# Small loads issued from GpSimd's queue, and the read-out of the memory's keys spread behind the first query unit in other PSUM banks: a one-core decoder trunk

## The chip, the core and the metric

The kernel runs on one NeuronCore of a Trainium2 chip. The metric is the device time of one execution in microseconds (us); the time of a kernel is the median of its runs. Engines are named as in the profile: PE (TensorE), DVE (VectorE), ACT (ScalarE), POOL (GpSimd) and SP (SyncE, which here only issues loads). Each engine, and each engine's queue of DMA issues, works through its own instructions in a fixed order.

## What is computed

One sandwich-normalised layer on 256 tokens of width 2048 in float32: the input is normalised and projected, four branches (causal pooling, dilated window attention, chunked gated linear attention, attention into 256 memory tokens) work on parts of the projection, sigmoid gates mix their outputs, and one output projection is normalised and added to the input.

```python
h = rms_norm(x, g_pre[l])
proj = h @ w_in[l]
(a_val, a_gate, sq, sk, sv, s_gate, cq, ck, cv, c_gate, c_lr,
 mq, m_gate, g_logits) = jnp.split(proj, split_at, axis=-1)
y_a = pool_mixer(a_val, a_gate, w_pool[l], pool_scale[l])
...
y_m = mem_attn(mq, m_gate, mem, g_mem[l], w_mem_kv[l])   # keys km, values vm = rms_norm(mem, g_mem) @ w_mem_kv
gates = jax.nn.sigmoid(g_logits.reshape(B, S, N_BRANCH, D_MODEL) + b_merge[l])
merged = (gates[:, :, 0] * (y_a @ w_br_pool[l]) + ... + gates[:, :, 3] * (y_m @ w_br_mem[l]))
x = x + rms_norm(merged @ w_out[l], g_post[l])
```

## The kernel before

Every float32 matmul operand is split in two: a high part (ACT copies the tile to the narrower matmul type) and a low part (DVE subtracts the high part from the tile). `split_w` (L134) does this for half a weight tile of 128x2048, which `load_raw` (L129) has fetched by SP's queue into one of 13 buffers (`raw`). Names end in `h` and `l` for the two parts: `cq10h` and `cq10l` are the first half of the unit `cq1`. High and low parts have five buffers each. PE then multiplies high by high, high by low and low by high.

A `b_unit` (L174) loads one weight tile, splits each half, and issues 16 matmuls a half, pairs of one with 512 and one with 256 columns; its result is read from PSUM by `two_sums` (L193): one copy on ACT (`cq1s`), one addition on DVE (`gq` for queries).

The head of the program, where most of the change lies:

- `mem_chunk(0)` to `mem_chunk(3)` (L305): the memory tokens (`mr`, with parts `mhl`) times the weights of the values (`vma`, two PSUM banks) and of the keys (`kma`, four banks). The sums of squares of the memory go to `msq`.
- `x_prep` (L286), woven in between by a list of generators (`queue`, of which `pull` runs one step): loads x in four tiles `xn`, adds up squares in `xsq`, works out the inverse norms (`inv_rms`, L244: matmuls `xpc`, a power on POOL, matmul `xpr`, a copy), scales x by 16 instructions of L297, and splits it into `xhl`.
- After chunk 3, L353 to L356 read out the four key banks (`km0s` to `km3s` with an addition each) and the two value banks.
- Then the query units `cq0` to `cq3` and the key units `ck0` to `ck3` (L640 on) of the linear attention, with three generators pulled in between: `bias_prep` (L384: POOL clears `braw`, SP loads the merge biases into it, `brow` and `sel` are made), `quarter_prep` (L362: eight differences `qs` of quarters of x, each split into a `quarter` tile, for the gate matmuls), and `m_norm` (L269: the memory's inverse norms `mcol` and `mrow`; `vm` and `km` are scaled by them). `drain("quarters")` before `ck0` runs what is left of the biases and quarters.
- From `ck0` on, the gate matmuls (`gu`, `gt`, `gv`, L409) fill PE between all other units.

SP also fetches `walpha` and `big_cst` (L480, L482; constants first used far later) and, near the end, the four pooling weights `wpr` (L805). The branch matmuls of the tail (`bmem`, `bswa`, ...) come from L902 on.

PSUM has the tags `sm` (2 banks), `acc` (2) and `seven` (4). Before, values lie in `seven`, keys in two `seven` and two `acc` banks; `b_unit` takes its bank from `acc`.

Of the kernel before, what the change touches and what calls it, by code (L numbers as in the profile page):

```python
# [8 lines left out]
F32 = mybir.dt.float32  # L9
R = mybir.dt.float32r  # L10
AF = mybir.ActivationFunctionType
ALU = mybir.AluOpType
# [25 lines left out]
def kernel(ctx, tc, ins, out):  # L38
# [83 lines left out]

    raw_count = [0]

    def new_raw():
        raw_count[0] += 1
        return e8(f"raw{raw_count[0]}", [P, 2048])

    def load_raw(src, n):  # L129
        raw = new_raw()  # L130
        sync.dma_start(raw[:, :n], src[:, :n])
        return raw

    def split_w(raw_ap, n, name):  # L134
        hi = wp.tile([P, 1024], R, tag="hi", bufs=NB_HILO, name=name + "h")
        lo = wp.tile([P, 1024], R, tag="lo", bufs=NB_HILO, name=name + "l")
        act.activation(hi[:, :n], raw_ap, AF.Copy)  # L137
        vec.tensor_tensor(lo[:, :n], raw_ap, hi[:, :n].bitcast(F32), op=ALU.subtract)
        return hi, lo

    def mm3(o, sh, sl, wh, wl, start=False, stop=False, again=False):
# [29 lines left out]

        return finish

    def b_unit(name, src, mov, evac):  # L174

        a = acc(f"{name}a", [P, 512])
        raw = load_raw(src, 2048)
        for hf in range(2):
            hi, lo = split_w(raw[:, hf * 1024 : (hf + 1) * 1024], 1024, f"{name}{hf}")
            for kk in range(8):  # L180
                k = 8 * hf + kk
                ws = slice(kk * P, (kk + 1) * P)
                mh, _ = mov(k)
                ten.matmul(a[:], lhsT=hi[:, ws], rhs=mov.both(k), start=(k == 0), stop=False)  # L184
                ten.matmul(a[:, :T], lhsT=lo[:, ws], rhs=mh, start=False, stop=(k == KT - 1))
            if hf == 0:
                pull(1)
                gates(2.8)
        evac(name, a)
        pull(1)  # L190
        gates(2.8)
# [48 lines left out]
    def fold(sq):  # L240
        vec.tensor_tensor(sq[:, 0, 0:2], sq[:, 0, 0:2], sq[:, 0, 2:4], op=ALU.add)
        vec.tensor_tensor(sq[:, 0, 0], sq[:, 0, 0], sq[:, 0, 1], op=ALU.add)

    def inv_rms(name, sq, col, row):  # L244

        fold(sq)
        yield
        pc = sm(f"{name}pc", [P, 2, 2])
        for t in range(2):
            ten.matmul(pc[:, t, :], lhsT=sq[:, 0, 0, t * P : (t + 1) * P], rhs=ones[:, 0:2], start=True, stop=True)  # L250
        vec.tensor_scalar(col, pc[:, :, 0], 1.0 / D, EPS, op0=ALU.mult, op1=ALU.add)
        pool.tensor_tensor(col, col, half[:], op=ALU.pow)
        dg = c2(f"{name}dg", [P, T])
        for t in range(2):
            vec.tensor_scalar(dg[:, t * P : (t + 1) * P], ident[:], col[:, t : t + 1], None, op0=ALU.mult)
        yield
        pr = sm(f"{name}pr", [P, T])
        ten.matmul(pr[:], lhsT=ones[:], rhs=dg[:], start=True, stop=True)
        vec.tensor_copy(row, pr[:])
# [7 lines left out]
    vm = c4("vm", [P, 2, 512])  # L267

    def m_norm():  # L269
        yield from inv_rms("m", msq, mcol[:], mrow)  # L270
        yield
        for t in range(2):
            act.activation(vm[:, t, :], vm[:, t, :], AF.Copy, scale=mcol[:, t : t + 1])
        yield
        for h in range(4):
            vec.tensor_tensor(km[:, h, :], km[:, h, :], mrow, op=ALU.mult)
        yield
# [8 lines left out]
    def x_prep():  # L286
        for c in range(4):
            xn.append(c4(f"xn{c}", [P, 4, T]))
            sync.dma_start(xn[c][:], ins["xT"][:, 4 * c : 4 * c + 4, :])
            squares(xsq, xn[c], c)  # L290
            yield
        yield from inv_rms("x", xsq, xcol[:], xrow)
        yield
        for c in range(4):
            for i in range(4):
                k = 4 * c + i
                vec.scalar_tensor_tensor(xn[c][:, i, :], xn[c][:, i, :], g_pre[:, k : k + 1], xrow,  # L297
                                         op0=ALU.mult, op1=ALU.mult)
            put_hilo(h_at.four(c, 0), h_at.four(c, 1), xn[c][:])
            yield  # L300

    vm_acc = [seven(f"vma{t}") for t in range(2)]
    km_acc = [seven(f"kma{h}") if h < 2 else acc(f"kma{h}", [P, 512]) for h in range(4)]

    def mem_chunk(c):  # L305

# [21 lines left out]
        for j in range(2048 // n):  # L328
            hi, lo = split_w(rv[:, j * n : (j + 1) * n], n, f"vm{c}{j}")
            for i in range(n // 512):  # L330
                k, ws = (n // 512) * j + i, slice(i * 512, (i + 1) * 512)
                for t in range(2):
                    ts = slice(t * P, (t + 1) * P)
                    mm3(vm_acc[t][:], hl[:, k, 0, ts], hl[:, k, 1, ts], hi[:, ws], lo[:, ws],
                        c == 0 and k == 0, c == 3 and k == 3)
            if n * (j + 1) % 1024 == 0:
                pull(1)
        squares(msq, rawx, c)
        for j in range(2):
            hi, lo = split_w(rk[:, 1024 * j : 1024 * j + 1024], 1024, f"km{c}{j}")  # L340
# [9 lines left out]
    queue.append(("xprep", x_prep()))  # L350
    for c in range(1, 4):
        mem_chunk(c)
    for h in range(4):  # L353
        two_sums(f"km{h}", km_acc[h], km[:, h, :])
    for t in range(2):
        act.activation(vm[:, t, :], vm_acc[t][:], AF.Copy)  # L356
    drain("xprep")


    quarter = [e8(f"quarter{i}", [P, 2, 8, P], R) for i in range(4)]  # L360
# [23 lines left out]
    def bias_prep():  # L384
        raw = c2("braw", [48, 512])
        pool.memset(raw[:], 0.0)
        rows = ins["b_merge"].rearrange("b (j c) -> (b j) c", c=512)
        sync.dma_start(raw[0:16, :], rows)
        sync.dma_start(raw[32:48, :], rows)
        act.activation(brow[:], raw[:], AF.Copy)  # L390
        vec.tensor_tensor(brow[32:48, :], raw[32:48, :], brow[32:48, :].bitcast(F32), op=ALU.subtract)
        one = c2("bsel", [48, 24])
        vec.tensor_tensor(one[:, 0:16], ident[0:48, 0:16], ident[0:48, 32:48], op=ALU.add)
        two = one[:, 0:16].rearrange("p (r i) -> p r i", i=2)
        vec.tensor_tensor(one[:, 16:24], two[:, :, 0], two[:, :, 1], op=ALU.add)
        vec.tensor_copy(sel[:], one[:])
        yield
# [70 lines left out]
    def all_gates():  # L468
        for jj in range(2):
            for b in range(4):  # L470
                yield from gate_pair(b, jj)

    queue.append(("quarters", bias_prep()))
    queue.append(("quarters", quarter_prep()))
    queue.append(("mnorm", m_norm()))
# [1 line left out]
    vec.tensor_scalar(g_gla, g_gla, 0.5, None, op0=ALU.mult)  # L477
    vec.tensor_scalar(p_scale, p_scale, 0.5, None, op0=ALU.mult)
    walpha = cst.tile([16, 512], F32, name="walpha")
    sync.dma_start(walpha[:], ins["w_alpha"])  # L480
    big_cst = cst.tile([P, 1344], F32, name="big_cst")
    sync.dma_start(big_cst[:], ins["consts"])  # L482
    dist0 = big_cst[:, 0:384].rearrange("p (g j) -> p g j", g=3)
    dist1 = big_cst[:, 384:1152].rearrange("p (g j) -> p g j", g=3)
    amask = big_cst[:, 1152:1280]
# [152 lines left out]
    vec.tensor_copy(ones_r[:], ones[:])  # L638

    for h in range(4):  # L640
        b_unit(f"cq{h}", ins["w_cqk"][h], h_at, plain_evac(gq[:, h, :], SCALE))
    drain("quarters")
    gate_stream[0] = all_gates()
    for h in range(4):
# [157 lines left out]

    def mix(g):
        wr = c2(f"wpr{g}", [P, 512])
        sync.dma_start(wr[:], ins["w_pool"][g])  # L805
        yield from pool_group(g)
        hi, lo = split_w(wr[:], 512, f"wpl{g}")
        yield
# [244 lines left out]
```

## Time and profile before

| | |
|---|---|
| median of 3 runs | 1206.92 us (1206.21 to 1209.74) |
| the profiled execution's own time | 1205.37 us |
| its span | 1203.5 us, so 1.9 us lie around it |
| instructions | 15395 |
| PE busy | 1161.6 us (97%), 5846 matmuls |
| DVE / ACT / POOL busy | 962.8 (80%) / 648.4 (54%) / 51.2 us (4%) |
| TensorE's granted clock over the span | 0.987 of full speed |
| DMA | 301.84 MB, 251 GB/s on average; SP's queue 62.3% of the 16 engines' time |
| chain that ended last | PE 69%, DVE 7%, DMA 5%, issue 2%, ACT 2% |

PE is busy for all but 42 us of the span. A gap is read in the view of waits and in the timeline: a number in brackets is how long the engine was idle before the row's instruction, and behind the arrow stands what ended that idle time. The clock is read in the windows (column PEclk) and in the distance between the starts of equal matmuls.

### The profile page before, as it was taken

What the parts mean: (1) busy time and instruction counts of PE and PEld (TensorE: products, weight loads), DVE (VectorE), ACT (ScalarE), POOL (GpSimd) and SP (SyncE); (2) the same over time, 40 slices, a digit from 0 to 9 for tenths busy, and PEclk for the clock granted to TensorE, in tenths of its full rate; (3) what the DMA queues carried; (4) which work ended last, traced back from release to release, by engine and by line L of the source; (5) the groups of instructions that cost most, each with busy time, mean ns of one, the idle gap of its engine ahead of it and who ended that gap; (6) DMA issues with size and microseconds to landing.
All of it is one profiled execution on the core that took longest, in us unless ns stands there. A gap on an engine that the chain in (4) does not pass through costs nothing.

```text
span 1203.5 us, 15395 instructions
## 1 busy us (share of the span) xinstructions
PE 1161.6 (97%) x5846; PEld 975.2 (81%) x5846; DVE 962.8 (80%) x1197; ACT 648.4 (54%) x823; POOL 51.2 (4%) x96
## 2 busy tenths in 40 slices
PE   9779999999999999999999999999999989999997
PEld 7558888878888878888888888888887868888787
DVE  6857978899799799789789968988987677776454
ACT  7455447475655655566566556556555443443341
POOL 0100000000101000000000000000000111110000
PEclk9889999999999999999999999999999989999999
DMA  9346768858877778688778767687769498649321
GB/s 357 123 185 245 247 208 295 297 189 295 292 262 253 272 270 308 226 289 286 249 255 284 240 232 271 241 283 266 257 243 367 137 388 349 252 167 395 116 71 71
DMA packets 79514, 301.84 MB, mean 251 GB/s; under 512 B 6176, under 2 KB 8608, under 8 KB 57040
## 3 DMA queue, kind: packets, MB, share of 16 engines
q1 hardware_dynamic: 66384, 270.29, 62.3%
q0 software_dynamic: 7728, 20.98, 5.0%
q10 hardware_dynamic: 5328, 9.60, 2.1%
q8 instruction: 46, 0.75, 0.2%
q14 instruction: 28, 0.23, 0.1%
HBM read 284.06 MB, written 16.78 MB: 250 GB/s over the span
## 4 chain that ended last, share of the span: by engine, by line
PE 69%; DVE 7%; DMA 5%; issue 2%; ACT 2%; DVEq 0%; POOLq 0%; POOL 0%; ACTq 0%
PE q L144 4%; PE q L143 4%; PE q L145 4%; DMA raw<-in_w_g 4%; PE p L143 2%; PE p L145 2%; PE p L144 2%; DVE raw L437 1%; PE sp L728 1%; PE sv1a L143 1%; PE sv2a L143 1%; PE o1a L144 1%; PE sv0a L143 1%; PE sv2a L145 1%; PE sv1a L145 1%
## 5 line engine op out<-in xcount | busy, mean ns | idle before, releaser
L437 DVE TENSOR_TENSOR raw<-raw 128x1024 f32<-128x1024 f32 x64 | 77.9, 1219 | 15.9 <-DMA raw<-in_w_g 15.9
L443 DVE TENSOR_TENSOR raw<-raw 128x512 f32<-128x512 f32 x64 | 43.9, 688 | 1.2
L438 DVE TENSOR_TENSOR raw<-raw 128x512 f32<-128x512 f32 x64 | 43.7, 685 | 0.6
L878 POOL DMA_DIRECT2D g<-gd x32 | 17.2, 537 | 107.3 <-DVE merged L886 70.1
L886 DVE TENSOR_TENSOR merged<-merged,g 128x512 f32<-128x512 f32 x24 | 15.4, 684 | 0.0
L655 POOL DMA_DIRECT2D cgd<-cgate x4 | 2.4, 590 | 251.6 <-DVE cgate L213 251.6
L736 ACT ACTIVATE s<-s,st 128x384 f32<-128x384 f32 (+1 forms) x8 | 6.2, 775 | 11.4 <-DVE st L735 11.4
L218 ACT ACTIVATE xhl<-xn 128x1024 fp32r<-128x1024 f32 x4 | 4.2, 1058 | 13.7 <-DVE xn L297 13.6
L760 POOL DMA_DIRECT2D ybd<-ybt x4 | 2.7, 682 | 185.4 <-DVE ybt L219 185.4
L933 DVE TENSOR_TENSOR yg<-o0a,gpost 128x512 f32<-128x512 f32 x2 | 1.4, 691 | 11.3 <-ACT oj L932 11.3
L728 PE MATMUL sp<-k,q 128*128 128x128 f32 (+1 forms) x48 | 9.7, 331 | 0.0
L728 PEld LDWEIGHTS sp<-k,q 128*128 128x128 f32 x48 | 7.2, 190 | 1.3 <-issue 0.6
L731 DVE SCALAR_TENSOR_TENSOR s<-big_cst,sp 128x128 f32<-128x128 f32 (+1 forms) x24 | 7.0, 347 | 1.5 <-PE sp L728 1.5
L405 ACT ACTIVATE c<-c 128x512 f32<-128x512 f32 x8 | 5.0, 628 | 5.5 <-DVE c L451 5.4
L184 PE MATMUL cq2a<-xhl,cq20h 128*128 128x512 f32 x8 | 4.9, 611 | 3.2 <-ACT cq20h L137 3.2
L899 ACT ACTIVATE mTh<-mtp 128x512 fp32r<-128x512 f32 x8 | 4.4, 596 | 6.4 <-PE mtp L897 6.4
L932 ACT ACTIVATE oj<-o0a 128x512 f32<-128x512 f32 x2 | 1.2, 597 | 11.9 <-PE o0a L145 11.9
L324 ACT ACTIVATE mhl<-mr,vecs 128x256 fp32r<-128x256 f32 x16 | 6.9, 495 | 0.6 <-DMA mr<-in_memT 0.6
L754 PE MATMUL po<-pt,sv 128*128 128x256 f32 x24 | 7.2, 380 | 0.0
L325 DVE SCALAR_TENSOR_TENSOR mhl<-mr,vecs,mhl 128x256 fp32r<-128x256 f32 x16 | 6.8, 478 | 0.4 <-ACT mhl L324 0.4
L143 PE MATMUL bswa0a<-bswa000h,yb 128*128 128x512 f32 x4 | 2.5, 670 | 4.7 <-ACT bswa000h L137 4.7
L184 PE MATMUL cq1a<-xhl,cq10h 128*128 128x512 f32 x8 | 4.5, 566 | 2.5 <-ACT cq10h L137 2.5
(4600 smaller groups left out, 4598.7 us busy)
## 6 DMA issues: line engine op xcount, KB each, us to landing
raw<-in_w_g SPq DMA_DIRECT2D x112, 1024.0 KB, 5.6
raw<-in_w_sqk SPq DMA_DIRECT2D x24, 1024.0 KB, 5.0
raw<-in_w_sv SPq DMA_DIRECT2D x12, 1024.0 KB, 5.1
raw<-in_w_out SPq DMA_DIRECT2D x12, 1024.0 KB, 8.4
raw<-in_w_cqk SPq DMA_DIRECT2D x8, 1024.0 KB, 6.4
raw<-in_w_cg SPq DMA_DIRECT2D x8, 1024.0 KB, 6.2
raw<-in_w_av SPq DMA_DIRECT2D x8, 1024.0 KB, 7.0
raw<-in_w_ag SPq DMA_DIRECT2D x8, 1024.0 KB, 6.9
```

The source lines that it names most:

```text
L143: ten.matmul(o, lhsT=sh, rhs=wh, start=start, stop=False, skip_group_check=again)
L144: ten.matmul(o, lhsT=sh, rhs=wl, start=False, stop=False, skip_group_check=again)
L145: ten.matmul(o, lhsT=sl, rhs=wh, start=False, stop=stop, skip_group_check=again)
L184: ten.matmul(a[:], lhsT=hi[:, ws], rhs=mov.both(k), start=(k == 0), stop=False)
L437: vec.tensor_tensor(r4[:, :, 0, :], r4[:, :, 0, :], r4[:, 1, :, :], op=ALU.add)
L438: vec.tensor_tensor(r4[:, 1, 1, :], r4[:, 1, 1, :], r4[:, 0, 0, :], op=ALU.add)
L443: vec.tensor_tensor(r4[:, 0, 1, :], r4[:, 0, 1, :], r4[:, 1, 1, :], op=ALU.add)
L728: ten.matmul(parts[g], lhsT=q3[:, g, it * P : (it + 1) * P], rhs=k3[:, g, :nj], start=True, stop=True)
L731: vec.scalar_tensor_tensor(s[:, g, :], dist[:, g, :], SLOPES[g * 4 + hh], parts[g], op0=ALU.mult, op1=ALU.add)
L754: ten.matmul(po[:], lhsT=sv[g][:, 0, vs], rhs=pt[g][:, 0:T], start=(g == 0), stop=False)
L878: pool.dma_start(gs[t][:], gate_dram[b, j, t][:])
L886: vec.tensor_tensor(m, m, gs[t][:], op=ALU.add)
```

## The change

Loads: `walpha`, `big_cst`, the two bias loads and the four `wpr` go from SP's queue to POOL's. PSUM: the values move to the two `acc` banks, the keys to the four `seven` banks. Order: the value banks are read out inside chunk 3; the keys are read out by a generator `km_evac`, first in the list, each step after `cq0`'s split; `cq0`'s load and split are done ahead of its unit (`b_split`); the folds of the squares (L240) leave `inv_rms`, and `m_norm`'s waits for `cq0`'s split.

```diff
     def split_w(raw_ap, n, name):
...
-        act.activation(hi[:, :n], raw_ap, AF.Copy)
-        vec.tensor_tensor(lo[:, :n], raw_ap, hi[:, :n].bitcast(F32), op=ALU.subtract)
+        last_split[0] = act.activation(hi[:, :n], raw_ap, AF.Copy).ins
+        last_split[1] = vec.tensor_tensor(lo[:, :n], raw_ap, hi[:, :n].bitcast(F32), op=ALU.subtract).ins
         return hi, lo
...
+    def b_split(name, src):
+        raw = load_raw(src, 2048)
+        return [split_w(raw[:, hf * 1024 : (hf + 1) * 1024], 1024, f"{name}{hf}") for hf in range(2)]
+
-    def b_unit(name, src, mov, evac):
+    def b_unit(name, src, mov, evac, ready=None):
 
         a = acc(f"{name}a", [P, 512])
-        raw = load_raw(src, 2048)
+        if ready is None:
+            raw = load_raw(src, 2048)
         for hf in range(2):
-            hi, lo = split_w(raw[:, hf * 1024 : (hf + 1) * 1024], 1024, f"{name}{hf}")
+            hi, lo = ready[hf] if ready else split_w(raw[:, hf * 1024 : (hf + 1) * 1024], 1024, f"{name}{hf}")
...
     def inv_rms(name, sq, col, row):
 
-        fold(sq)
-        yield
...
     def m_norm():
+        with tc.issue_after(cq0_split[1]):
+            fold(msq)
+        yield
         yield from inv_rms("m", msq, mcol[:], mrow)
...
             squares(xsq, xn[c], c)
             yield
+        fold(xsq)
+        yield
         yield from inv_rms("x", xsq, xcol[:], xrow)
+        yield
         yield
...
-    vm_acc = [seven(f"vma{t}") for t in range(2)]
-    km_acc = [seven(f"kma{h}") if h < 2 else acc(f"kma{h}", [P, 512]) for h in range(4)]
+    vm_acc = [acc(f"vma{t}", [P, 512]) for t in range(2)]
+    km_acc = [seven(f"kma{h}") for h in range(4)]
...
+        if c == 3:
+            for t in range(2):
+                act.activation(vm[:, t, :], vm_acc[t][:], AF.Copy)
         squares(msq, rawx, c)
...
-    for h in range(4):
-        two_sums(f"km{h}", km_acc[h], km[:, h, :])
-    for t in range(2):
-        act.activation(vm[:, t, :], vm_acc[t][:], AF.Copy)
+
+    def km_evac():
+        for h in range(4):
+            with tc.issue_after(cq0_split[0]), tc.issue_after(cq0_split[1]):
+                two_sums(f"km{h}", km_acc[h], km[:, h, :])
+            yield
+
     drain("xprep")
+    cq0 = b_split("cq0", ins["w_cqk"][0])
+    cq0_split = tuple(last_split)
...
-        sync.dma_start(raw[0:16, :], rows)
-        sync.dma_start(raw[32:48, :], rows)
+        pool.dma_start(raw[0:16, :], rows)
+        pool.dma_start(raw[32:48, :], rows)
...
+    queue.append(("kmevac", km_evac()))
     queue.append(("quarters", bias_prep()))
...
-    sync.dma_start(walpha[:], ins["w_alpha"])
+    pool.dma_start(walpha[:], ins["w_alpha"])
     big_cst = cst.tile([P, 1344], F32, name="big_cst")
-    sync.dma_start(big_cst[:], ins["consts"])
+    pool.dma_start(big_cst[:], ins["consts"])
...
-        b_unit(f"cq{h}", ins["w_cqk"][h], h_at, plain_evac(gq[:, h, :], SCALE))
+        b_unit(f"cq{h}", ins["w_cqk"][h], h_at, plain_evac(gq[:, h, :], SCALE), cq0 if h == 0 else None)
...
-        sync.dma_start(wr[:], ins["w_pool"][g])
+        pool.dma_start(wr[:], ins["w_pool"][g])
```

Where this moves instructions. A row is the line of the kernel it is from, the operation, what it writes and reads (with buffer numbers), and the size.

ACT before, from the end of `cq1` (its copy `cq1s`) to the first gate weights; `quarter_541` to `quarter_544` are the four quarter tiles:

```order
L196 ACTIVATE cq1s<-cq1a 128x256
L218 ACTIVATE quarter_543<-qs_619 128x512
L218 ACTIVATE quarter_544<-qs_620 128x512
L137 ACTIVATE cq20h<-raw_677 128x1024
L137 ACTIVATE cq21h<-raw_677 128x1024
L137 ACTIVATE cq30h<-raw_733 128x1024
L137 ACTIVATE cq31h<-raw_733 128x1024
L137 ACTIVATE ck00h<-raw_788 128x1024
L196 ACTIVATE cq2s<-cq2a 128x256
L218 ACTIVATE quarter_541<-qs_725 128x512
L137 ACTIVATE gu0000h<-raw_815 128x1024
```

ACT with the change, from the end of `cq2` (its copy `cq2s`) to the same place; the four quarter tiles are now `quarter_539` to `quarter_542`:

```order
L203 ACTIVATE cq2s<-cq2a 128x256
L225 ACTIVATE quarter_539<-qs_709 128x512
L225 ACTIVATE quarter_540<-qs_710 128x512
L281 ACTIVATE vm<-vm,mcol 128x512 x2
L139 ACTIVATE cq30h<-raw_717 128x1024
L139 ACTIVATE cq31h<-raw_717 128x1024
L203 ACTIVATE cq3s<-cq3a 128x256
L225 ACTIVATE quarter_541<-qs_711 128x512
L225 ACTIVATE quarter_542<-qs_712 128x512
L225 ACTIVATE quarter_539<-qs_771 128x512
```

After these ten come `quarter_540<-qs_772`, `quarter_541<-qs_773` and `quarter_542<-qs_774`, and only then `ck00h`. So the splits of `cq3` and of `ck0`, which stood ahead of `cq2s`, stand behind it: `cq30h` behind two quarters and the scaling of `vm`, `ck00h` behind `cq3s` and six more quarters.

DVE with the change, from `cq2`'s sum to the splits of `cq3`, with the memory's norm `mcol` behind the first quarter's low part:

```order
L207 SCALAR_TENSOR_TENSOR gq<-cq2a,cq2s 128x256
L388 TENSOR_TENSOR qs_710<-xn_239,qs_709 128x512
L226 TENSOR_TENSOR quarter_539<-qs_709,quarter_539 128x512
L256 TENSOR_SCALAR mcol<-mpc 128x2
L226 TENSOR_TENSOR quarter_540<-qs_710,quarter_540 128x512
L140 TENSOR_TENSOR cq30l<-raw_717,cq30h 128x1024
```

Before, `mcol` stood ahead of `cq0`, and `cq30l` followed the splits of `cq2` directly.

DVE with the change, from `cq3`'s sum (the row `gq<-cq3a,cq3s`) to the split of `ck0`:

```order
L207 SCALAR_TENSOR_TENSOR gq<-cq3a,cq3s 128x256
L388 TENSOR_TENSOR qs_712<-xn_284,qs_710 128x512
L226 TENSOR_TENSOR quarter_541<-qs_711,quarter_541 128x512
L388 TENSOR_TENSOR qs_771<-xn_258,xn_308 128x512
L226 TENSOR_TENSOR quarter_542<-qs_712,quarter_542 128x512
L388 TENSOR_TENSOR qs_772<-xn_258,qs_771 128x512
L226 TENSOR_TENSOR quarter_539<-qs_771,quarter_539 128x512
L388 TENSOR_TENSOR qs_773<-xn_258 128x512
L226 TENSOR_TENSOR quarter_540<-qs_772,quarter_540 128x512
L388 TENSOR_TENSOR qs_774<-xn_308,qs_772 128x512
L226 TENSOR_TENSOR quarter_541<-qs_773,quarter_541 128x512
L226 TENSOR_TENSOR quarter_542<-qs_774,quarter_542 128x512
```

The next row is `ck00l`. Before, `ck00l` stood ahead of `cq2`'s sum on DVE, and the quarters after it alternated with splits of gate weights.

SP's queue before, from the load of `cq0`'s tile (the first row), with the bias loads ahead of the tiles of `cq1`, `cq2`, `cq3` and `ck0`:

```order
L131 DMA raw_562<-in_w_cqk 128x2048
L388 DMA braw<-in_b_merge 16x512
L389 DMA braw<-in_b_merge 16x512
L131 DMA raw_625<-in_w_cqk 128x2048
L131 DMA raw_677<-in_w_cqk 128x2048
L131 DMA raw_733<-in_w_cqk 128x2048
L131 DMA raw_788<-in_w_cqk 128x2048
```

With the change the same five tiles follow each other, and the bias loads stand in POOL's queue:

```order
L133 DMA raw_529<-in_w_cqk 128x2048
L133 DMA raw_602<-in_w_cqk 128x2048
L133 DMA raw_654<-in_w_cqk 128x2048
L133 DMA raw_717<-in_w_cqk 128x2048
L133 DMA raw_788<-in_w_cqk 128x2048
```

On ACT and DVE the parts of chunk 3 (`mhl`, `vm30`, `vm31`) also move ahead of the scaling of x, and on PE the small matmuls of the memory's norm (`mpc`) and of two biases move from ahead of chunk 3's values and behind `cq0` to behind `cq2`.

## Rows read from the trace of the kernel before

**Rows 1.** The view of windows: for a stretch its length, each engine's busy time (and instructions), TensorE's granted clock, the DMA engines' share and GB/s. Three stretches: the end of the query units, the gates, and the first swa block of the tail.

```profile
90.00:100.00 10.00, 10.00 (x52) 8.63 (x52) 6.30 (x9) 4.26 (x6) 0.00 (x0) 0.85 0.48 193
110.00:120.00 10.00, 10.00 (x52) 8.41 (x51) 7.77 (x11) 5.24 (x7) 0.00 (x0) 1.00 0.86 315
970.00:980.00 10.00, 9.06 (x27) 6.77 (x28) 7.41 (x9) 5.66 (x7) 1.07 (x2) 0.66 1.01 420
```

**Rows 2.** The view of waits of PE over the whole span: who waits, for what; us in total, times, longest.

```profile
PE bswa0a L143 <- ACT bswa000h L137: 4.7, 1, 4.7
PE vma L143 <- ACT vm30h L137: 3.9, 1, 3.9
PE cq2a L184 <- ACT cq20h L137: 3.2, 1, 3.2
PE vma L144 <- DVE vm30l L138: 3.1, 1, 3.1
PE cq1a L184 <- ACT cq10h L137: 2.5, 1, 2.5
...
PE cq0a L184 <- DVE km L198: 0.6, 1, 0.6
```

**Rows 3.** The timeline of PE from the end of chunk 2 to the first key unit: start, duration, instruction, idle time before it.

```profile
43.53 0.50 PE L250 MATMUL mpc<-ones,msq 128*128 128x2 f32 x4
...
51.72 0.79 PE L144 MATMUL vma<-vm30l,mhl 128*128 128x512 f32 x1 [3.07 <-DVE vm30l L138]
...
58.55 0.39 PE L345 MATMUL kma<-mhl,km30h 128*128 128x512 f32 x1
...
65.32 0.28 PE L185 MATMUL cq0a<-xhl,cq00l 128*128 128x256 f32 x1
...
75.29 0.38 PE L185 MATMUL cq1a<-xhl,cq10l 128*128 128x256 f32 x1 [0.76 <-DVE cq10l L138]
...
82.22 0.28 PE L185 MATMUL cq1a<-xhl,cq11l 128*128 128x256 f32 x1
...
86.96 0.58 PE L185 MATMUL cq2a<-xhl,cq20l 128*128 128x256 f32 x1 [0.76 <-DVE cq20l L138]
...
95.12 0.39 PE L184 MATMUL cq3a<-xhl,cq30h 128*128 128x512 f32 x1
95.36 0.27 PE L185 MATMUL cq3a<-xhl,cq30l 128*128 128x256 f32 x1
...
100.90 0.27 PE L185 MATMUL ck0a<-xhl,ck00l 128*128 128x256 f32 x1
```

**Rows 4.** The timeline of ACT: the last part of x, the scaling of `vm`, and what follows the end of `cq1`.

```profile
56.29 1.06 ACT L218 ACTIVATE xhl<-xn 128x1024 fp32r<-128x1024 f32 x1 [4.31 <-DVE xn L297]
...
61.38 0.74 ACT L273 ACTIVATE vm<-vm,mcol 128x512 f32<-128x512 f32 x1
...
82.60 0.38 ACT L196 ACTIVATE cq1s<-cq1a 128x256 f32<-128x256 f32 x1 [7.67 <-PE cq1a L185]
82.88 0.62 ACT L218 ACTIVATE quarter<-qs 128x512 fp32r<-128x512 f32 x1
84.07 0.63 ACT L218 ACTIVATE quarter<-qs 128x512 fp32r<-128x512 f32 x1 [0.57 <-DVE qs L369]
84.61 1.04 ACT L137 ACTIVATE cq20h<-raw 128x1024 fp32r<-128x1024 f32 x1
```

**Rows 5.** The timeline of DVE: the last split of chunk 2, seven scalings of x, the last low part of x, and what follows the end of `cq1`.

```profile
34.99 1.21 DVE L138 TENSOR_TENSOR km21l<-raw,km21h 128x1024 fp32r<-128x1024 f32 x1
...
41.41 2.86 DVE L297 SCALAR_TENSOR_TENSOR xn<-xn,vecs,xsq 128x256 f32<-128x256 f32 x7
...
57.38 1.23 DVE L219 TENSOR_TENSOR xhl<-xn,xhl 128x1024 fp32r<-128x1024 f32 x1
...
83.01 0.42 DVE L200 SCALAR_TENSOR_TENSOR gq<-cq1a,cq1s 128x256 f32<-128x256 f32 x1 [6.04 <-ACT cq1s L196]
83.36 0.68 DVE L369 TENSOR_TENSOR qs<-xn,qs 128x512 f32<-128x512 f32 x1
83.95 1.47 DVE L219 TENSOR_TENSOR quarter<-qs,quarter 128x512 fp32r<-128x512 f32 x2
```

**Rows 6.** The waits of SP's queue (the bias loads), the timeline of SP where the four query and key tiles follow them, and the timeline of POOL (the power of the memory's norm).

```profile
SPq L388 <- POOL braw L386: 29.0, 1, 29.0
...
60.54 6.36 SPq L131 DMA_DIRECT2D raw<-in_w_cqk  x4
...
57.54 1.63 POOL L252 TENSOR_TENSOR mcol<-mcol,half 128x2 f32<-128x2 f32 x1 [18.62 <-DVE mcol L251]
```

**Rows 7.** The list of DMA issues (KB each, median us from issue to landing), and two windows of the head with columns as in the first group.

```profile
raw<-in_w_cqk SPq DMA_DIRECT2D x8, 1024.0 KB, 6.4
...
big_cst<-in_consts SPq DMA_DIRECT2D x1, 672.0 KB, 13.0
...
0.00:10.00 10.00, 7.48 (x32) 6.01 (x33) 4.70 (x11) 5.72 (x11) 1.33 (x9) 1.00 0.78 255
10.00:20.00 10.00, 9.90 (x50) 8.00 (x49) 8.04 (x11) 9.16 (x13) 0.00 (x0) 1.00 1.03 411
```

**Rows 8.** The timeline of ACT in the tail, ahead of the first split of the block `bswa0`.

```profile
968.70 0.63 ACT L218 ACTIVATE plh<-pl 128x512 fp32r<-128x512 f32 x1 [3.62 <-DVE pl L797]
969.80 1.06 ACT L137 ACTIVATE bswa000h<-raw 128x1024 fp32r<-128x1024 f32 x1 [0.47 <-DMA raw<-in_w_br_swa]
```

More of the change, by code (lines that the diff above doesn't have):

```diff
@@ L123 @@
     raw_count = [0]
+    last_split = [None, None]
     def new_raw():
```

## The prediction, as recorded before the changed kernel ran

> **What bounds the kernel now.** The page comes first: PE is busy for 97% of the span, so only its gaps, and the stretches in which its clock is low, can give time. The waits of PE come second [rows 2]: the largest are one in the tail (`bswa0a`, 4.7 us) and a family in the head, `vma` 3.9 and 3.1, `cq1a` 2.5, `cq2a` 3.2 and `cq0a` 0.6; the timeline adds 0.76 each for the low parts of `cq1` and `cq2` [rows 3]. In the head these are 14.8 us of idle PE between 43.5 and 100.9 us. Third comes the clock. From 95.36 to 100.90 lie 32 matmuls (16 pairs) without a wait, 5.54 us, or 0.35 a pair; that is the 2.4 GHz level. From the second matmul of `cq2` at 86.96 to the same place of `cq3` at 95.36 the same number took 8.40 [rows 3], and the window around it has a granted clock of 0.85 [rows 1]: behind the gap part of the unit ran at 1.2 GHz, which cost 2.9 us. In the same way `cq1` (75.29 to 82.22, 6.93 against 5.19 for its 30 steps) lost 1.7, and chunk 3 (51.72 to 58.55, 6.83 for 22 matmuls of 512 columns, against 5.0 at two thirds of a pair each) lost 1.8. So the head pays 14.8 of idle time and 6.4 of clock. From the gates on PE is full at clock 1.00 [rows 1]: lateness at the first gate weights is not caught up there.
>
> The reader is to see who ends the waits of `cq1` and `cq2`: not a load but ACT's split, which stands in order behind the unit before it: copy `cq1s`, two quarters, then `cq20h` [rows 4]. Loads are not what PE waits for here; the place of a split in ACT's and DVE's order is, and the change moves those places.
>
> **The change, part by part.** Times are those of the profiled execution (1205.37 us), which is 1.55 below the median shown (1206.92); differences carry over.
>
> *Chunk 3.* The memory's parts go ahead of the scaling of x on ACT and DVE, so `vm30l` is ready before PE ends chunk 2 at 43.5. The waits of 3.9 and 3.1 and the clock loss of 1.8 go.
>
> *`cq0`.* What is late next is DVE, which has the same work to do and PE no longer slower. From the end of `km21l` at 36.2 [rows 5] it has to do: the memory's low parts (4 at 0.40, as the scalings, 7 in 2.86), the norm's small steps and copy (1.0), four splits and a square sum of chunk 3 (5 at 1.14, start to start), 16 scalings (6.4), four low parts of x (4.6) and `cq00l` (1.2): 20.5, so 56.7 without a wait. The last part of x waits for ACT's copy (1.06 [rows 4]), and the norm crosses POOL and PE, some 0.8: I take 58.6 for the second matmul of `cq0`, against 65.32 [rows 3]: 6.7 earlier. PE, done with the keys at about 55.3 (24 matmuls at 0.23 and 16 pairs at 0.35 from 43.5, and half a us for the last low part), waits 3 us in two pieces; the gap is shaped like that of `cq1`, so I take its clock loss, 1.7 (bounds 0, as behind the 0.6 of `cq0` before, and 2.9). `cq0` ends at 58.6 + 5.3 + 1.7 = 65.6.
>
> *`cq1`, `cq2`.* Their tiles no longer queue behind the bias loads, for which SP sat 29.0 us [rows 6], and their splits follow `cq01h` directly. Their waits go. At 5.55 each, `cq2` ends at 76.7; before it was 95.12 [rows 3]. Here the change is 18.4 us ahead. The small matmuls moved behind `cq2` fall into the next gap.
>
> *`cq3`.* On ACT `cq30h` now stands behind `cq2s`, two quarters and two scalings of `vm`, and these behind `mcol`, which on DVE stands behind the first quarter's low part. From the end of a unit, in the rows of `cq1` (end about 82.33): the sum starts after 0.7, `qs` after 1.0, the low part after 1.6 [rows 5]; so `mcol` after 2.2, POOL's power after 2.4 for 1.0 to 1.6 us (1.63 in its row [rows 6]), two scalings at 0.62 [rows 4] to 4.8 to 5.3, `cq30h` 1.09 and `cq30l` 1.26. First matmul 6.2 after `cq2`, second 7.4 (in the old order `cq2` had 3.4 and 4.6 after `cq1`). The second starts at 84.1. The gap is longer than any in the head, so I take the largest loss, 2.9. `cq3` ends at 84.1 + 5.3 + 2.9 = 92.3.
>
> *`ck0`.* `ck00h` stands behind six quarters, whose differences begin on DVE behind `cq3`'s sum: nine instructions of 0.59 (start to start, 83.36 to 83.95 [rows 5]) from 1.0 to 6.4, ACT's quarter to 6.9, `ck00h` to 8.0, `ck00l` to 9.3. Before, `ck0` had no wait at all, since `ck00h` was done before `cq2` ended. The second matmul of `ck0` starts at 92.3 + 9.3 = 101.6 against 100.90 [rows 3]: all 18.4 us are spent. Behind a gap of 9 us the clock falls once more, where it was full before: 2.9. The gates are 0.7 + 2.9 = 3.6 later.
>
> *Early loads.* `big_cst` (672 KB) was issued behind the first chunks [rows 7]; from POOL it goes out in the first microseconds, while PE already lacks work (7.48 of 10 us) and the DMA engines move 255 GB/s. At the 411 GB/s of the next window [rows 7] it takes 1.7 us of the engines. Its cover is whatever slack the head keeps: bounds 0 and 1.7, and I take half, 0.8, since nothing shown says which loads it delays.
>
> *Biases, weights of pooling.* The biases wait only for POOL's clearing; `brow` follows `cq1`: nothing, covered by the gap at `cq3`. SP's waits for `wpr` go, so the tiles of `bswa` come earlier. But `bswa000h` stands behind `plh` on ACT, and only 0.47 us of its wait ended with the load [rows 8]: gain 0.5, bounds 0 and 7.6 (the whole 4.7 [rows 2] and 2.9 of clock, granted 0.66 there [rows 1]).
>
> Sum: 3.6 + 0.8 - 0.5 = 3.9 slower, 1209.3 for a profiled execution like that of before, 1210.8 by the median.
>
> **The rivals.** *A, the queue does it (faster).* The two new waits are only half as long, because the quarters are worked off while PE is still in `cq2` and `cq3`. Then the second matmul of `cq3` starts at 76.7 + 3.7 = 80.4, the unit ends at 80.4 + 5.3 + 1.7 = 87.4 (loss as at `cq1`, whose gap was as long), `ck0` has its second matmul at 92.1 and loses 1.7: 7.2 ahead of before, with the early loads and the tail -7.2 + 0.8 - 0.5 = -6.9, 1200.0. It decides as soon as the two waits of 7.4 and 9.3 are together a quarter shorter. For it: SP's 29 us, the largest wait of the head, does go. Against: before, `cq20h` started at 84.61 behind a quarter [rows 4], long after its tile, one of the four issued from 60.54 to 66.9 and 6.4 us on the way [rows 6, 7]; and the order of ACT and DVE fixes both chains.
>
> *B, the clock stays (faster or no change).* If the three gaps don't lower it, 1.7 + 2.9 + 2.9 fall out of the sum: 3.9 - 7.5, 1203.3. For it: behind `cq0`'s 0.6 us nothing was lost. Against: every gap of 3 us and more in the head was followed by a slow stretch [rows 1, 3].
>
> *C, nothing moves.* The lead of 18.4 and the new waits cancel: with the low bounds (no loss at `cq0`, 1.7 in place of 2.9 at `ck0`, no early load) 3.6 - 1.7 - 1.2 - 0.5 is 0.2, 1207.1. The Trainium skill ("Trainium Kernel Development and Optimization", Key Constraints) speaks for this: loads issued by SP, ACT and POOL run on the same 16 DMA engines, and issuing from several only saves issue time. By that rule the moved loads gain next to nothing. The row of SP's 29.0 us [rows 6] speaks against the rule's "only", since that was no issue time but order in a queue; but a load that comes early for a split that comes late gains nothing either.
>
> *D, the early load costs all.* All 1.7 of `big_cst` shift the first chunks, and `cq0` loses 2.9: 3.6 + 1.2 + 1.7 - 0.5 = 6.0, 1212.9.
>
> **How the numbers follow.** This kernel's runs tell 0.3% (3.6 us) from no change: below 1203.3 is faster, above 1210.5 slower. Forecast 0.55, and since it lies near that bound, 0.42 of it slower and 0.13 the same; its own range is 1208.5 to 1213.5. A 0.14 (0.13 faster, 0.01 the same), B 0.08 (half and half), C 0.17 (the same), D 0.06 (slower). Together faster 0.17, same 0.35, slower 0.48. The range reaches from 1202.5, below B, to 1213.5, above D; A's part below and what lies beyond D leave out less than 0.2.
>
> **What would show it.** Right: no wait at `vma`, `cq1a` and `cq2a`; `cq2` ends near 77; waits before `cq3a` of about 6 in the first and 1 in the second matmul, before `ck0a` of 8 and 1; clock below 1.00 after each; `ck0`'s second matmul near 101.6; SP's wait for `braw` gone; `bswa0a` still at 4 or more. Wrong, if `cq30h` starts less than 3 us after `cq2`'s end, if `ck0a` shows no wait, if the clock is 1.00 behind gaps of 6 to 9 us, or if the tail's wait is gone.

## The result: slower by 0.38%

The changed kernel took 1210.26 us (median of 20 runs, 1206.34 to 1215.35), the kernel before 1205.14 us beside it (20 runs, 1201.59 to 1210.02). The ratio is 1.0038 with a 95% interval of 1.0025 to 1.0050, that is 4.6 us (3.0 to 6.0). Forecast were 1210.8 us and 3.9 us; the 1210.8 was counted from the 1206.92 us of three earlier runs of the kernel before, so the differences, 3.9 and 4.6, are what to compare. The profiled execution took 1207.70 us, near the lower end of the runs (span 1205.5, granted clock 0.984).

### The profile after

The waits of PE over the whole span, to be held against [rows 2]:

```profile
PE ck0a L191 <- ACT ck00h L139: 8.0, 1, 8.0
PE cq3a L191 <- ACT cq30h L139: 4.8, 1, 4.8
PE bswa0a L145 <- ACT bswa000h L139: 4.3, 1, 4.3
PE cq0a L191 <- ACT cq00h L139: 1.9, 1, 1.9
...
PE cq0a L192 <- DVE cq00l L140: 0.9, 1, 0.9
...
PE ck0a L192 <- DVE ck00l L140: 0.5, 1, 0.5
PE cq3a L192 <- DVE cq30l L140: 0.5, 1, 0.5
```

The waits of the head that [rows 2, 3] show are gone: `vma`'s 3.9 and 3.1, those of `cq1` and `cq2`, and the 0.6 ahead of `cq0`. (Smaller ones in the first chunks are still there; the one for `vm01h` is 1.6 where it was 0.7.) In their place stand three others (first and second matmul taken together): `cq0` with 2.8, `cq3` with 5.3 and `ck0` with 8.5, in all 16.6 us against 14.8. (At `cq3` PE also works off the small matmuls that were moved there.)

The timeline of PE, to be held against [rows 3]:

```profile
60.61 0.39 PE L192 MATMUL cq0a<-xhl,cq00l 128*128 128x256 f32 x1 [0.94 <-DVE cq00l L140]
...
77.43 0.50 PE L255 MATMUL mpc<-ones,msq 128*128 128x2 f32 x4
77.86 0.50 PE L419 MATMUL p<-brow,sel 48*128 48x512 f32 x1
...
83.41 0.80 PE L191 MATMUL cq3a<-xhl,cq30h 128*128 128x512 f32 x1 [4.82 <-ACT cq30h L139]
84.67 0.58 PE L192 MATMUL cq3a<-xhl,cq30l 128*128 128x256 f32 x1 [0.46 <-DVE cq30l L140]
...
92.10 0.28 PE L192 MATMUL cq3a<-xhl,cq31l 128*128 128x256 f32 x1
100.39 0.79 PE L191 MATMUL ck0a<-xhl,ck00h 128*128 128x512 f32 x1 [8.02 <-ACT ck00h L139]
101.65 0.58 PE L192 MATMUL ck0a<-xhl,ck00l 128*128 128x256 f32 x1 [0.47 <-DVE ck00l L140]
...
106.46 0.40 PE L145 MATMUL p<-gu0000h,xhl 128*128 128x512 f32 x1
```

`cq2` ends at 77.43, 17.7 us ahead of before (95.12), and `ck0` has its second matmul at 101.65, 0.75 behind (100.90). Then 4.81 us pass to the first gate matmul, where before it was 2.54 (100.90 to 103.44): the clock is low again. The gates begin 3.0 us late.

Who ends these waits: ACT from the end of `cq2`, to be held against [rows 4].

```profile
77.63 0.39 ACT L203 ACTIVATE cq2s<-cq2a 128x256 f32<-128x256 f32 x1 [4.48 <-PE cq2a L192]
77.91 0.62 ACT L225 ACTIVATE quarter<-qs 128x512 fp32r<-128x512 f32 x1
79.11 0.63 ACT L225 ACTIVATE quarter<-qs 128x512 fp32r<-128x512 f32 x1 [0.57 <-DVE qs L388]
81.08 1.33 ACT L281 ACTIVATE vm<-vm,mcol 128x512 f32<-128x512 f32 x2 [1.34 <-POOL mcol L257]
82.32 1.04 ACT L139 ACTIVATE cq30h<-raw 128x1024 fp32r<-128x1024 f32 x1
...
92.47 0.38 ACT L203 ACTIVATE cq3s<-cq3a 128x256 f32<-128x256 f32 x1 [8.17 <-PE cq3a L192]
...
98.77 0.63 ACT L225 ACTIVATE quarter<-qs 128x512 fp32r<-128x512 f32 x1 [0.57 <-DVE qs L388]
99.30 1.04 ACT L139 ACTIVATE ck00h<-raw 128x1024 fp32r<-128x1024 f32 x1
```

`cq30h` sits behind the power on POOL and two scalings, `ck00h` behind six quarters, the later of which each wait 0.57 us for a difference on DVE. No load ends any of these waits: the tile of `cq3` was issued at 45.8 us and took 5.0 to land, that of `ck0` at 61.7 and took 4.7, so both lay ready over 30 us before their splits. The windows of the same stretches [rows 1]:

```profile
80.00:90.00 10.00, 6.13 (x19) 4.87 (x20) 3.42 (x4) 3.23 (x4) 2.08 (x3) 0.66 0.29 105
90.00:100.00 10.00, 2.38 (x14) 1.82 (x12) 7.01 (x12) 4.66 (x8) 0.00 (x0) 0.81 0.00 0
100.00:110.00 10.00, 9.14 (x32) 7.32 (x33) 7.96 (x8) 6.82 (x8) 0.00 (x0) 0.68 0.51 184
```

From 90 to 100 us PE works 2.38 of 10 us. The DMA engines stand still there: the tiles have long come.

The loads: SP's queue no longer waits for the bias, and its five tiles go out one after the other between 32.8 and 62.0 us; POOL issues `big_cst` in the third microsecond; DVE's last split of chunk 2 comes at 37.03 instead of 34.99 [rows 5].

```profile
32.76 29.28 SPq L133 DMA_DIRECT2D raw<-in_w_cqk  x5
```

```profile
2.35 0.57 POOL L502 DMA_DIRECT2D big_cst<-in_consts  x1
```

```profile
37.03 1.22 DVE L140 TENSOR_TENSOR km21l<-raw,km21h 128x1024 fp32r<-128x1024 f32 x1
```

In the tail `bswa000h` follows `plh` at once on ACT, without the 0.47 us for its tile [rows 8], and PE's wait is 4.3 in place of 4.7:

```profile
969.61 0.63 ACT L225 ACTIVATE plh<-pl 128x512 fp32r<-128x512 f32 x1 [3.85 <-DVE pl L817]
970.15 1.04 ACT L139 ACTIVATE bswa000h<-raw 128x1024 fp32r<-128x1024 f32 x1
```

### The profile page after: what moved, and what is told of

Read it like the earlier page. It is cut to its first block, busy times and chain, and to the rows that moved or that the text cites. A ratio compares the mean times of both kernels' runs of the same rounds, so it can differ in the third digit from the quotient of the medians.

```text
span 1205.5 us, 15389 instructions
## 1 busy us (share of the span) xinstructions
PE 1162.7 (96%) x5846; PEld 976.3 (81%) x5846; DVE 962.2 (80%) x1197; ACT 649.6 (54%) x823; POOL 55.3 (5%) x104
## 5 line engine op out<-in xcount | busy, mean ns | idle before, releaser
L191 PE MATMUL ck0a<-xhl,ck00h 128*128 128x512 f32 x8 | 5.2, 648 | 8.0 <-ACT ck00h L139 8.0
L756 ACT ACTIVATE s<-s,st 128x384 f32<-128x384 f32 (+1 forms) x8 | 6.2, 774 | 11.8 <-DVE st L755 11.8
L191 PEld LDWEIGHTS ck0a<-xhl,ck00h 128*128 128x128 f32 x8 | 2.6, 325 | 8.9 <-ACT ck00h L139 8.3
L191 PE MATMUL cq3a<-xhl,cq30h 128*128 128x512 f32 x8 | 5.2, 645 | 4.8 <-ACT cq30h L139 4.8
L424 ACT ACTIVATE c<-p 128x512 f32<-128x512 f32 x8 | 4.7, 592 | 5.1 <-PE p L147 5.1
L191 PEld LDWEIGHTS cq3a<-xhl,cq30h 128*128 128x128 f32 x8 | 2.6, 326 | 5.8 <-ACT cq30h L139 5.3
```

What stands on the lines that cost most here:

```text
L424: act.activation(dst, src, AF.Tanh, scale=0.5)
```

## The experiments

The theory: the place of each split in ACT's and DVE's order is what PE waits for; the moved loads are not, apart from the early `big_cst`, which delays the first chunks; and a lag at the first gate weights stays to the end. The rivals: SP's wait of 29 us held the query units; or the gate stream gives a lag back. Ratios are to the kernel before, run beside each.

### The two halves of the change

Only the queues, in the kernel before (queues_only):

```diff
-    sync.dma_start(walpha[:], ins["w_alpha"])
+    pool.dma_start(walpha[:], ins["w_alpha"])
```

and the same for `big_cst`, the two bias loads and the `wpr` load.

> The kernel before with nothing changed but the queue of the eight small loads (POOL in place of SP). Theory 1 (the place of each split in ACT's and DVE's order is what PE waits for, and the early big_cst load delays the first chunks): the waits of PE at cq1 (2.5 and 0.8) and cq2 (3.2 and 0.8) stay as before within 0.2, although the four tiles arrive some 15 us earlier; the first chunks come 2.0 later, as in the changed kernel (km21l on DVE at 37.0 in place of 35.0); time 0 to 2 us above before, ratio 1.000 to 1.002. Rival (SP's wait of 29 us is what held the query units): the waits at cq1 and cq2 go, and the time falls by 5 us or more, ratio below 0.996.

Measured: 1207.17 us, ratio 1.0013 (1.0003 to 1.0023). The waits:

```profile
PE cq2a L184 <- ACT cq20h L137: 3.2, 1, 3.2
...
PE cq1a L184 <- ACT cq10h L137: 2.5, 1, 2.5
...
PE cq2a L185 <- DVE cq20l L138: 0.8, 1, 0.8
```

At the query units they are those of before to the tenth ([rows 2]; only `cq1`'s low part is 0.5 in place of 0.8, as in the second profile of the unchanged kernel), although SP's queue no longer waits for the biases. It waits at other places instead: the tiles of `cq1` and `cq2` landed 22 and 5 us earlier than before (43.6 and 63.1 us), those of `cq3` and `ck0` 1 to 2 us later, so the 15 us that were expected of all four were not met. But the two units that wait had their tiles earlier and waited as long. `km21l` came at 37.04. The rival of the queue falls: taking SP's wait away gained nothing at the query units, and the moved loads together cost 1.6 us (0.4 to 2.8).

Only the order, banks and read-out, with all eight loads on SP (order_only):

```diff
-    pool.dma_start(walpha[:], ins["w_alpha"])
+    sync.dma_start(walpha[:], ins["w_alpha"])
```

and so on for the other seven, in the changed kernel.

> The changed kernel with all eight small loads back on SP: only the order of the read-out, the folds, the early split of cq0 and the PSUM banks remain. Theory 1: the waits of the changed kernel at cq3 (4.8 and 0.5) and ck0 (8.0 and 0.5) stay within 0.3, because ACT's and DVE's orders are the same; without the early load the first chunks are 2.0 earlier, and the second matmul of ck0 starts at 99.5 to 100 in place of 101.65; time 1 to 2.5 us below the changed kernel, ratio to before 1.001 to 1.003. Rival (the moved loads cause the loss): ratio 1.000 or below, with shorter waits at cq3 and ck0.

Measured: 1208.60 us, ratio 1.0022 (1.0010 to 1.0035). The waits:

```profile
PE ck0a L191 <- ACT ck00h L139: 8.0, 1, 8.0
...
PE cq3a L191 <- ACT cq30h L139: 4.4, 1, 4.4
```

`ck0`'s second matmul started at 100.22, 1.4 earlier than in the changed kernel; part of the 2.0 us went to the clock behind `cq0`, which fell here. (The wait at `cq3` is 0.4 shorter than expected.) The order alone makes the kernel slower; how much of that belongs to the banks, the folds or the read-out was not tested.

Only `walpha` and `big_cst` back on SP, in the changed kernel (the same edit for these two lines; consts_on_sp):

> The changed kernel with walpha and big_cst alone back on SP; bias loads and the pooling weights stay on POOL. Theory 1: the whole 2.0 us of the early chunks come from big_cst, so the head and the time are those of order_only within 1 us (ratio to before 1.001 to 1.003), with km21l on DVE at 35.0 and the wait at vm01h back from 1.6 to 0.7. Rival (the bias loads or the pooling weights do the harm, or the early load is hidden): time as the changed kernel, ratio 1.0038.

Measured: 1207.95 us, ratio 1.0021 (1.0007 to 1.0034), as order_only. `km21l` came at 34.71. So the delay of the first chunks comes with these two loads, of which `big_cst` has 672 KB and `walpha` only 16x512 values (it was not moved alone). In time the intervals of this version and of the changed kernel overlap (1.0007 to 1.0034, 1.0025 to 1.0050): the delay of 2.0 is shown in the profiles, its worth at the end, about 2 us by the medians, only roughly. The bias loads and the pooling weights make no difference that these runs can tell.

### The splits put ahead

In the changed kernel, each unit's load and splits written one unit earlier (splits_ahead):

```diff
+    split = cq0
     for h in range(4):
-        b_unit(f"cq{h}", ins["w_cqk"][h], h_at, plain_evac(gq[:, h, :], SCALE), cq0 if h == 0 else None)
+        ahead = b_split(f"cq{h + 1}" if h < 3 else "ck0", ins["w_cqk"][h + 1])
+        b_unit(f"cq{h}", ins["w_cqk"][h], h_at, plain_evac(gq[:, h, :], SCALE), split)
+        split = ahead
     drain("quarters")
...
-        b_unit(f"ck{h}", ins["w_cqk"][4 + h], h_at, plain_evac(gk[:, h, :]))
+        b_unit(f"ck{h}", ins["w_cqk"][4 + h], h_at, plain_evac(gk[:, h, :]), split if h == 0 else None)
```

> The changed kernel with the load and split of each query unit, and of ck0, written one unit earlier: on ACT and DVE the splits of cq3 then stand ahead of cq1's read-out, the splits of ck0 right behind cq3's. Theory 1: the wait at cq3 (4.8 and 0.5) is gone, that at ck0 falls from 8.0 and 0.5 to about 1.7 and 0.9; the quarters now stand ahead of gu0000l on DVE, which costs PE 3 to 5.5 us there; the gates start 7 to 9 us earlier than before, and if lateness and lead at the gates are both kept to the end, as the prediction held, the time is 7 to 9 us below before, ratio 0.9925 to 0.994. Rival (what happens in the head is mostly given back in the gate stream between 120 and 260 us, as the trace of the changed kernel suggests, where a lag of 3.8 at cv1a was 1.1 at cg10a and 0.1 at bswa): the time is within 3 us of before, ratio 0.9975 to 1.001, with the same lead at ck0.

Measured: 1199.06 us, ratio 0.9946 (0.9931 to 0.9961). The waits of PE between 55 and 110 us:

```profile
PE p L145 <- ACT gu0000h L139: 1.9, 1, 1.9
PE cq0a L191 <- ACT cq00h L139: 1.9, 1, 1.9
PE cq0a L192 <- DVE cq00l L140: 1.0, 1, 1.0
PE ck0a L192 <- DVE ck00l L140: 0.8, 1, 0.8
PE p L146 <- DVE gu0000l L140: 0.8, 1, 0.8
PE p L145 <- ACT p1c L445: 0.7, 1, 0.7
```

The 5.3 us at `cq3` are gone and the 8.5 at `ck0` are 0.8 (the small matmuls of `mpc` and the biases fill the first part of that gap); the quarters now hold `gu0000` for 2.7. One edit of order thus turns 4.6 us of loss into 6.5 us of gain (a little less than expected), and what it took away at `cq3` and `ck0` is more than the loss.

The same edit in the kernel before, with nothing else of the change (before_ahead):

> The kernel before, with the loads on SP, the old PSUM banks, the old read-out and the old folds, and only the splits written one unit earlier (cq0 to cq3, ck0), as in splits_ahead. Theory 1 (what counts is where a split stands in ACT's and DVE's order, not the moved loads): cq10h now stands behind cq01h, ahead of cq0's read-out, so the wait at cq1 (2.5, 0.8) and its clock loss of 1.7 go; cq20h stands right behind cq1's copy, so the wait at cq2 falls from 3.2 and 0.8 to about 1.7 and 0.9; chunk 3's 3.9 and 3.1 stay; cq3 and ck0 have no wait; the gates start 5 to 8 us earlier and the lead is kept: ratio 0.9935 to 0.996. Rival (the queue move or the early read-out is needed, since SP sits 29 us and the tile of cq1 comes at 67 us): the wait at cq1 stays above 2 us, now ended by the load, and the ratio is above 0.998.

Measured: 1198.81 us, ratio 0.9944 (0.9928 to 0.9959). The waits between 60 and 110 us:

```profile
PE cq2a L189 <- ACT cq20h L137: 0.8, 1, 0.8
PE cq2a L190 <- DVE cq20l L138: 0.8, 1, 0.8
PE cq0a L189 <- DVE km L203: 0.6, 1, 0.6
```

```profile
30.00 3.88 SPq L131 DMA_DIRECT2D raw<-in_w_cqk  x2
59.59 0.33 SPq L393 DMA_DIRECT2D braw<-in_b_merge  x1
...
60.48 7.43 SPq L131 DMA_DIRECT2D raw<-in_w_cqk  x3
```

SP's queue still stands before the bias load until 59.59, and the tiles of `cq2`, `cq3` and `ck0` still come after it. (The edit does put the load of `cq1`'s tile ahead of the biases, at 33.6 in place of 60.5; queues_only had that tile early too, and `cq1` waited all the same.) The gates began at 93.93 in place of 103.44, and the gain is that of splits_ahead. Where the splits stand was enough; neither the queue without the biases nor the other banks were needed, and once the splits stand ahead the rest of the change makes no difference that these runs can tell (0.9946 with it, 0.9944 without).

splits_ahead with `walpha` and `big_cst` on SP (ahead_consts_sp):

> splits_ahead with walpha and big_cst back on SP's queue behind the weights of chunk 3: both costs of the change removed. Theory 1 (order and early load are independent costs of the head, and a lead is kept to the end, as in splits_ahead): km21l 2.0 earlier, the lead at ck0a 16 us in place of 14.3; 1 to 2 us below splits_ahead, ratio to before 0.993 to 0.9945. Rival (the 2.0 us are absorbed by a wait at the first gate weights): the same as splits_ahead, 0.9946, with a longer wait at gu0000.

Measured: 1196.67 us, ratio 0.9942 (0.9923 to 0.9962). `ck0` began at 85.04 in place of the 86.41 of splits_ahead. The interval covers both the theory and the rival: whether 1 to 2 us come on top can't be told.

ahead_consts_sp, with the key banks also read two per step, so the quarters come earlier (quarters_spread):

```diff
                 two_sums(f"km{h}", km_acc[h], km[:, h, :])
-            yield
+            if h % 2:
+                yield
```

> ahead_consts_sp with the key banks read two per step in place of one, so that the quarters begin two steps earlier. In ahead_consts_sp PE still waits 2.0 and 0.8 at gu0000, 0.8 at ck0a and 0.7 at p1c, behind quarters on DVE. Theory 1: these waits shrink to under 1.5 in all, but cq30h now stands behind cq2's copy, which brings 1.7 and 1.2 at cq3; the gates start 0 to 2 us earlier than in ahead_consts_sp, ratio to before 0.9925 to 0.9942. Rival (the wait only moves to cq3, with a clock loss of 1.7 or 2.9 behind it): no gain, 0.9942 to 0.9965.

Measured: 1195.03 us, ratio 0.9923 (0.9902 to 0.9945), the lowest of all, though its interval overlaps those of the other versions with the splits ahead. Waits between 55 and 110 us:

```profile
PE cq0a L191 <- ACT cq00h L139: 1.9, 1, 1.9
PE cq0a L192 <- DVE cq00l L140: 0.9, 1, 0.9
PE cq3a L192 <- DVE cq30l L140: 0.8, 1, 0.8
PE p L145 <- ACT p1c L446: 0.7, 1, 0.7
```

`gu0000` has no wait left, and at `cq3` 0.8 came where 2.9 were expected: the small matmuls of `mpc` and the biases stand ahead of `cq3` on PE and fill the first part; the clock fell behind it all the same (granted 0.72 in the 6 us from `cq3`'s start). The gates began at 89.32 against 103.44, 14.1 earlier, more than expected. This profile, the fastest of the six runs, ended 13.0 us before that of the kernel before (spans 1190.5 and 1203.5); by the medians the gain is 9.3 us (6.6 to 11.8).

### Is a lag at the gates kept?

The two profiles seemed to deny the prediction's last step. The changed kernel was 3.8 us behind at `cv1` (172.1 against 168.3), but only 1.1 at `cg10` (251.4 against 250.3) and 0.3 at `bswa0` (971.2 against 970.9). To test it, the kernel before got 16 needless matmuls on PE and nothing else (pe_late):

```diff
+            if name == "cq3" and hf == 0:
+                for k in range(8):
+                    ws = slice(k * P, (k + 1) * P)
+                    ten.matmul(a[:], lhsT=hi[:, ws], rhs=mov.both(k), start=(k == 0), stop=False)
+                    ten.matmul(a[:, :T], lhsT=lo[:, ws], rhs=mov(k)[0], start=False, stop=(k == 7))
```

> The kernel before with the 16 matmuls of the first half of cq3 issued twice (the second pass starts the sum anew): 2.8 us more work on PE alone, just ahead of ck0; all other orders are those of before. It asks what a lag at the first gate weights is worth at the end. Theory 1 (the gate stream between 160 and 260 us has waits of its own, 1.0 at gt103al and 0.8 at gt100al and more at 160 to 200, which a late PE doesn't meet, so part of a lag is given back): the lag is 2.8 at ck1a, 0.5 to 1.5 at cg10a and at the end; time +0.5 to +1.5, ratio 1.0004 to 1.0013, and the waits at gt100al and gt103al are gone. Rival (the prediction's assumption: lateness at the gates is not caught up): +2.8, ratio 1.0023, lag 2.8 at cg10a.

Measured: 1207.81 us, ratio 1.0028 (1.0019 to 1.0037), 3.4 us (2.3 to 4.5) for 2.8 us of work. My theory of this run fell: the lag was 2.6 at `ck1` and 2.8 at `cg10`, and the waits meant to absorb it were still there:

```profile
PE q L144 <- DVE gt103al L138: 1.0, 1, 1.0
PE q L144 <- DVE gt100al L138: 0.8, 1, 0.8
```

(In the second profile of the kernel before neither of them is there, so they decide little.) Later in the profile the lag is smaller, 1.2 at `bswa0` (972.1 against 970.9), which is as much as two profiles of the kernel before differ by there; the timed runs show it whole. A lag on PE at the gates is kept, as the prediction had it.

### The same two kernels again

> The kernel before, unchanged, for a second profile. In its first profile the granted clock stayed at 1.00 behind the wait of 1.7 and 0.5 us at o1a, in those of all changed kernels it fell there, at 1.6 to 1.7 us. Theory 1 (whether the clock falls behind a gap of this size differs from run to run): the waits agree with the first profile within 0.3, and the second matmul of ck0 starts within 0.5 of 100.90; the clock may fall at o1a. Rival (the clock's fall at o1a comes with the change): it stays at 1.00 there.

> The changed kernel, unchanged, for a second profile: its first profile took 1207.70 us, its 20 runs had a median of 1210.26. Theory 1 (the waits at cq3 and ck0 are fixed by the order, and what differs from run to run lies in the gate stream and in the clock behind the gaps): 4.8, 0.5, 8.0 and 0.5 again within 0.3, the second matmul of ck0 within 0.7 of 101.65, the lag to before at cg10a between 1 and 4 us. Rival (the head itself differs between runs): the second matmul of ck0 is 2 us or more away from 101.65.

Measured: 1205.23 and 1208.49 us, one run each. The waits of the head agreed (5.3 at `cq3`, 8.5 at `ck0`). But the second profile of before began its gates at 104.66 in place of 103.44, and was 1.0 us *ahead* of the first at `mq0` (314.0 against 315.0); the second of the changed kernel had `ck0`'s second matmul at 103.81, 2.2 behind the first, and was 4.8 behind the first of before at `mq0` (319.8). So the expectation for `ck0` (within 0.7 of 101.65) fell, as did that for the kernel before (102.06, where 0.5 around 100.90 was expected), and so did the story that the gate stream pays lags back: two profiles of one kernel differ there by as much as the effect itself. What differed in the head of the changed kernel is the clock behind `cq0`. The windows of the first 6 us of `cq0`, of the first and of the second profile of the changed kernel:

```profile
59.16:65.16 6.00, 5.05 (x27) 4.18 (x28) 6.00 (x9) 5.08 (x6) 0.00 (x0) 1.00 0.39 131
```

```profile
59.33:65.33 6.00, 5.05 (x18) 4.12 (x19) 6.00 (x9) 4.26 (x6) 0.00 (x0) 0.72 0.41 128
```

The gap ahead was the same (1.93 and 0.94, 1.90 and 0.95); in one run 27 matmuls began in these 6 us, in the other 18.

## Why the prediction was right

- **What bounds the head.** Right, and shown by both halves: the order alone costs 2.6 us (1.2 to 4.2), the queues alone gain nothing at the units that waited, and moving the splits ahead gains 6.5 and 6.7 us, in either kernel.
- **`cq0`.** The second matmul was put at 58.6 before the early load; it came at 60.61, and 2.0 of that is the early load (58.56 in order_only and 58.26 in consts_on_sp, which don't have it). The clock loss, put at 1.7, was 0 in the first profile (`cq1` began 5.5 after) and 1.5 in the second (7.03 from 60.78 to `cq1` at 67.81). In the five other profiles with this gap it was 1.5 in three and 2.5 in two, so the term was fair and the first profile the exception.
- **`cq1`, `cq2`.** No waits; end 76.7 forecast without the early load, 77.43 measured in the first profile. That is luck: the 2.0 of the early load came on top and the 1.7 of the clock fell out. In the second profile the unit ended at 79.13.
- **`cq3`.** First and second matmul 6.2 and 7.4 after `cq2`'s end forecast, 5.98 and 7.24 measured; from there to the unit's end at 92.21 (its last matmul began at 92.10) 7.55, so a clock loss of 2.2 against the 5.3 of a unit at full clock, where 2.9 was taken.
- **`ck0`.** 8.0 and 9.3 forecast; 8.2 and 9.4 measured from `cq3`'s end. Clock loss 2.3 to the first gate matmul (4.81 against 2.54), where 2.9 was taken. The gates were 3.0 late in the first profile, 5.2 in the second (108.67), each against the first of before (103.44; its second had 104.66); forecast 4.4 with the early load.
- **The early load** is the term that was mis-sized: 0.8 taken, bounds 0 and 1.7. The first chunks came 2.0 later, above the upper bound. In time the two versions without it are 0.16 to 0.17% below the changed kernel (1.0022 and 1.0021 against 1.0038), about 2 us, with intervals that overlap. No slack of the head covered the delay; the window with PE busy for 7.48 of 10 us [rows 7] had hinted at that. The error was made good by the clock losses at `cq3` and `ck0`, each 0.6 to 0.7 too large, so that the total came as close as 3.9 to 4.6 is in part luck.
- **The tail.** 0.5 forecast, 0.4 measured in both profiles (waits of 4.3). It does not follow from the moved loads alone: in queues_only the 0.47 for the tile went too, but `plh` came later and PE waited 4.8.
- **Kept to the end.** Assumed from full PE and clock 1.00 behind the head; shown by the needless matmuls for a lag of 2.8. A lead is less well measured: of the 14.1 us at the gates of quarters_spread its own profile kept 13.0, the medians give 9.3.
- **The rivals.** A fell, as both waits came at full length; what A promised comes with the splits ahead, not with the queue. B fell: the clock fell behind both long gaps in both profiles, and behind `cq0`'s in the second. C's time was wrong. The rule it drew on (the Trainium skill, "Trainium Kernel Development and Optimization", Key Constraints: loads from several queues run on the same DMA engines, and issuing from several saves only issue time) agrees with queues_only as far as nothing was gained there (1.0013); that SP's 29 us went as well shows that a queue can change without PE noticing. D came nearest to the size of the early load (1.7 for 2.0), but the clock loss of 2.9 at `cq0` came in neither profile of the changed kernel, and its total of 6.0 lies at the upper end of the interval.

## What to carry to other kernels

Ask of a moved instruction not only what it lets start earlier but what it lands ahead of on its in-order engine: here the 14.8 us of waits taken from some units came back as 16.6 at others, because the quarters and scalings had to be passed somewhere, and of the versions tried only those that write the next unit's split ahead of them were faster. A load that waited long in its queue cost nothing here while its consumer waited for something else; look at what ends the consumer's idle time. And a load issued early is not free where the first work already waits for data.

## What the runs showed that was not expected

Whether TensorE's clock falls from 2.4 to 1.2 GHz behind a gap of about 2 us is not fixed by the kernel. At `o1a` the wait is 1.7 and 0.5 us in all twelve profiles; in the 6 us from there the granted clock was 0.72 in nine of them and 1.00 in three, among them one of each kernel that was profiled twice:

```profile
1128.27:1134.27 6.00, 5.47 (x16) 4.05 (x17) 5.75 (x5) 4.52 (x5) 0.00 (x0) 0.72 0.40 94
```

```profile
1130.70:1136.70 6.00, 5.47 (x23) 4.24 (x24) 6.00 (x6) 4.78 (x5) 0.00 (x0) 1.00 0.36 100
```

(the first and the second profile of the changed kernel). The same held at `ag11a` (waits of 1.0 and 0.8; 0.72 in seven, 1.00 in five) and behind `cq0`'s 1.9 and 0.8 to 1.0 (a fall in six of seven). One fall cost 1.5 to 2.5 us behind `cq0`, and the 20 runs of the kernel before lie up to 8.4 us apart, for whatever cause, so a profile's own time is no measure of an effect of this size. The gaps of 4.3 us and more, at `cq3` and `ck0` in the kernels that have them and at `bswa0` in all, were followed by a fall every time.
